# Gates of 16 expert blocks applied where they are built, gate loads on the rows' queue, the gathered tile's remainder 48 rows later

## The chip, the core and the metric

The kernel runs on one core of a Trainium2 chip. The metric is device time in microseconds, the median of several executions. DVE is VectorE, ACT is ScalarE, PE is TensorE, POOL is GpSimd and SP is SyncE, an engine that here only issues transfers.

## The reference, cut to what matters

One decoder block over 512 tokens of 1024 values: a mixer (gated DeltaNet and mLSTM heads), cross-attention into 256 memory tokens, and a PEER layer, each added to the stream, then a last RMSNorm. The change touches the PEER layer alone. It picks for each token and each of 8 heads 16 of 128 x 128 = 16384 single-neuron experts, and computes

```
sc       = q . sub_keys                                  (two halves of 128 keys per head)
top 16 of each half -> 256 candidates -> top 16: expert_id, best_v
gate     = softmax(best_v)                               per head, 16 values
act      = gelu(u[expert_id] . h)                        u: 16384 x 1024, exact gelu
out      = sum over the 128 picked experts of gate * act * v[expert_id]
result   = rmsnorm(x + out) * norm_final_w
```

## The kernel before, in words

The 512 tokens are four tiles of 128. The mixer and the attention run on all tiles (to about 640 us). In the PEER layer the tiles are treated in two ways at the same time.

**Two gathered tiles (0 and 1; G0 in the code).** For each of its 128 slots (8 heads x 16 picks) a tile fetches one row of 1024 float32 per token, 512 KB per fetch, with an indirect DMA that POOL issues (`fetch`, L1057). A first pass over both tiles takes rows of u: DVE multiplies each by the tile's `hn` and sums (L1086). A second pass takes rows of v: DVE adds the row, times the slot's weight, into `hn` (L1097, L1099). That is 4 x 128 = 512 rows. `late_` (L1062) says at which slot of the next tile's pass a tile's remainder stands in the text: `weights_` (Gelu on ACT, L1066, and the product with the gates on DVE, L1067) after the u pass, and `close` (L1069) after the v pass. `close` loads x and the norm row on POOL's queue into two of the row buffers (L1072, L191), adds on DVE (L1074), squares on ACT (L1076) and scales on DVE (L1077); the result is stored later (L1106, L1108). Rows are counted here from 0 to 511 in text order, so `close` of the first tile stands after row 256 + 128 + 16 = 400.

**Two dense tiles (2 and 3, 256 tokens).** They take all 16384 experts, in 128 blocks of 128, which form 16 groups of eight (GB). For block n, TensorE multiplies the block of u with the tokens (16 matmuls of 128 x 256, L313), ACT applies Gelu and writes the activation into a slot of `room` (L961, called from `act_`), the activation is multiplied by a gate matrix that is zero where an expert was not picked (`gated`, L986, one DVE instruction of 128 x 2048 for eight blocks), and TensorE adds the block's part of the output into four PSUM banks (eight matmuls of 128 x 512, L989, called from `add`). `room` holds six groups, so activations run 47 blocks (AHEAD) ahead of additions.

The gate matrices are made tile by tile in 16 calls of `build` (L926), one for 16 tokens: DVE makes one-hot operands, TensorE multiplies them (L942), ACT copies the result into one of two stage buffers (L943) and stores it to DRAM (`gates_`, L944). They come back in groups of eight blocks into one of three buffers `gb` that lie in the same memory as the stages (`gates_of`, L981, issued by SP).

**The dense loop** (`peer_dense`, L963, L1004) has 128 steps e. Step e computes the activation of block e + 47 while there is one (steps 0 to 80), adds block e, issues the loads of a later row block of u (`in_pt`) and of v (`in_pv`), 512 KB each, on SP's queue into nine shared buffers, and runs some rows of the two gathered tiles: 3.3 per step (ROWS_BOTH) up to step 80 and 1.6 (ROWS_DOWN) after. Before the loop stand the first gate loads and `gated(0)` and `gated(1)`; group g + 2 is gated at step 8g + 5.

**What stands before the loop** is written out by hand in ORDER_XA (L56): u, t, T are routing of the dense tiles, b and B the two tiles' eight builds each, aN runs N activations ahead of the loop (47 in all), pN runs N rows of the gathered tiles (167 in all).

**What sets the order.** The text gives each engine's work and its priority; the compiler's planner then puts each instruction into its engine's stream by its own estimate of when operands and buffers are ready. An engine executes its stream strictly in order. Semaphores between the streams are all that holds at run time.

Of the kernel before, what the change touches and what calls it, by code (L numbers as in the profile page):

```python
# [6 lines left out]
F32 = mybir.dt.float32  # L7
# [5 lines left out]
OP = mybir.AluOpType  # L13
# [3 lines left out]
P = 128  # L17
# [11 lines left out]
K = 16  # L29
NSL = PH * K  # L30

ROWS_BOTH, ROWS_DOWN = 3.3, 1.6
NKEY = 128

GSCALE = 2.0 ** 15
# [20 lines left out]
ORDER_XA = ("w2 n0 q008 n1 s0 x0 s1 x1 q104 o0 w1 i0 q148 f0 f1 r6 "  # L56
            "f2 s2 p2 f3 s3 p4 x2 p3 r3 p2 r3 k0 x3 p4 o1 p8 i1 e0 R3 p4 R3 p2 R4 k1 "
            "u0 p5 u1 p5 u2 p5 a1 u3 p5 a2 "
            + "t2 p4 a1 " * 4 + "t2 p4 a5 " + "b1 p5 a1 T2 " * 4 + "b1 p5 a1 T2 a4 d0 " + "b1 p5 a2 " * 3
            + "B1 p5 a1 " * 8 + "a2 p3 " * 6)  # L60


class Phase:
# [12 lines left out]
def _body(ctx, tc, A, out, dbg):  # L76
    from contextlib import ExitStack
    nc = tc.nc
    V, SC, PE, G = nc.vector, nc.scalar, nc.tensor, nc.gpsimd

    def pool(name, bufs=1, **kw):
        return ctx.enter_context(tc.tile_pool(name=name, bufs=bufs, **kw))

    per = pool("per", 2)
    dram = pool("dram", 1, space=bass.MemoryType.DRAM)
# [831 lines left out]
    T = len(DENSE) * P  # L917
    NLD = 9
    TG, TS = 16, 8
    GB = 8  # L920
    NROOM = 6
    AHEAD = NROOM * GB - 1

    gates_ = dram.tile([NKEY // GB, P, T // TG, GB, TG], F32, name="gates_")

    def build(t0, bufs, stage, bank):  # L926

        for s in range(0, TG, TS):
            ts = slice(t0 + s, t0 + s + TS)
            oj, oi, og = hot(bufs())  # L930
            key = [slot[:, x, ts].rearrange("p (a q) -> p a q", q=Q).unsqueeze(2) for x in range(2)]
            for o, k in ((oj, key[1]), (oi, key[0])):
                V.tensor_tensor(o, ioq.unsqueeze(1).to_broadcast([P, TS // Q, P, Q]),
                                k.to_broadcast([P, TS // Q, P, Q]), op=OP.is_equal)
            gates = slot[:, 2:4, ts].rearrange("p g (a q) -> p g a q", q=Q)
            for a in range(TS // Q):
                V.tensor_tensor(og[:, :, a], oi[:, a].unsqueeze(1).to_broadcast([P, 2, P, Q]),
                                gates[:, :, a].unsqueeze(2).to_broadcast([P, 2, P, Q]), op=OP.mult)
                ps = bank()
                for k in range(Q):  # L940
                    for g in range(2):
                        PE.matmul(ps[:, k], oj[:, a, :, k], og[:, g, a, :, k], start=g == 0, stop=g == 1)  # L942
                SC.activation(stage[:, :, s + a * Q:s + a * Q + Q], ps.rearrange("p t i -> p i t"), AF.Copy, scale=1.0 / GSCALE)  # L943
        nc.scalar.dma_start(gates_[:, :, t0 // TG].rearrange("g p i t -> p g (i t)"),  # L944
                            stage.rearrange("p (g i) t -> p g (i t)", i=GB))

    NHOT = TS * 4 * P

# [6 lines left out]
    room, count_a = [], [0]  # L955

    def place(e):
        return room[e // GB % NROOM][:, e % GB]

# [3 lines left out]
    def peer_dense(wu, psO, psC, rest):  # L963
        h = second.h

        def load(src):
            t = wu.tile([P, D], F32, name="ld", bufs=NLD)
            nc.sync.dma_start(t, src)
            return t

        def loaded_u(e):
            return load(A["pt"][e].rearrange("p a b -> p (a b)")) if e < NKEY else None

        def loaded_v(e):
            return load(A["pv"][e * P:(e + 1) * P, :]) if e < NKEY else None

        gb = up_.rearrange("p a b -> p (a b)").rearrange("p (z c e t) -> p z c e t", z=3, c=T // TG, e=GB)

        def gates_of(g):
            if g < NKEY // GB:  # L980
                nc.sync.dma_start(gb[:, g % 3], gates_[g])  # L981

        def gated(g):

            a = room[g % NROOM].rearrange("p e (c t) -> p c e t", t=TG)
            V.tensor_tensor(a, a, gb[:, g % 3], op=OP.mult)  # L986

        def add(e, v, i, z):
            PE.matmul(outs[DENSE[i]][z], place(e)[:, i * P:(i + 1) * P], v[:, z * 512:(z + 1) * 512],  # L989
                      start=e == 0, stop=e == NKEY - 1)  # L990

        for ti in DENSE:
            outs[ti] = [psO.tile([P, 512], F32, name=f"o{ti}{z}") for z in range(2)]
        gates_of(0)
        us, vs = [], []
        for k in range(2):
            us.append(loaded_u(AHEAD + k))
            vs.append(loaded_v(k))
        for g in (1, 2):
            gates_of(g)  # L1000
        for g in (0, 1):
            gated(g)
        last, steps = [], 0
        for e in range(NKEY):  # L1004
            n = e + AHEAD
            if n < NKEY:
                ps = psC.tile([P, 512], F32, name="pa")[:, :T]
                times(us.pop(0).rearrange("p (a b) -> p a b", a=DB), h, ps)
            v = vs.pop(0)
            if e < NKEY - 1:  # L1010
                for i in range(len(DENSE)):
                    for z in range(2):
                        add(e, v, i, z)
            else:
                last.append((e, v))
            if n < NKEY:
                act_(n, ps)
            if e % GB == 5 and e + 2 * GB < NKEY:
                gated(e // GB + 2)
                gates_of(e // GB + 3)  # L1020
            us.append(loaded_u(n + 2))
            vs.append(loaded_v(e + 2))
            steps += ROWS_BOTH if n < NKEY else ROWS_DOWN
            run(rest, int(steps))
            steps -= int(steps)
        run(rest)

        n = len(DENSE)

        def plain():  # L1030
            return wu.tile([P, D], F32, name="ld", bufs=NLD)
        w = row_(4, plain())
        xs = [load(out[ti * P:(ti + 1) * P, :]) for ti in DENSE]
        junk = plain()
        ss = sm.tile([P, n, 2], F32, name="fss", bufs=1)
        half = [slice(z * 512, z * 512 + 512) for z in range(2)]
        rs = []
        for i, x in enumerate(xs):
            for z, c in enumerate(half):
                for e, v in last:  # L1040
                    add(e, v, i, z)
                V.tensor_tensor(x[:, c], outs[DENSE[i]][z], x[:, c], op=OP.add)
                SC.activation(junk[:, c], x[:, c], AF.Square, accum_out=ss[:, i, z:z + 1])
            if i:
                k = len(rs)
                t = sm.tile([P, n], F32, name="ft", bufs=1)
                V.tensor_tensor(t[:, k:i + 1], ss[:, k:i + 1, 0], ss[:, k:i + 1, 1], op=OP.add)
                r = rstd(t[:, k:i + 1], i + 1 - k, "n" if k == i else f"f{k}", 1.0 / D)
                for j in range(k, i + 1):
                    rs.append(r[:, j - k:j - k + 1])  # L1050
                    for c in half:
                        V.scalar_tensor_tensor(xs[j][:, c], xs[j][:, c], rs[j], w[:, c], op0=OP.mult, op1=OP.mult)
                        nc.sync.dma_start(out[DENSE[j] * P:(DENSE[j] + 1) * P, c], xs[j][:, c])

    def peer_gather(ready, buffer):

        def fetch(table, ids, s):  # L1057
# [1 line left out]
            G.indirect_dma_start(out=row, out_offset=None, in_=A[table],  # L1059
                                 in_offset=bass.IndirectOffsetOnAxis(ap=ids[:, s:s + 1], axis=0))  # L1060
            return row
        late_ = 16  # L1062

        def weights_(ti):

# [14 lines left out]
        act, done, stored = {}, [], []  # L1080
# [10 lines left out]
        for ti in G0:  # L1091
            hn, ids = first.hn[ti], first.ids[first.tiles.index(ti)].rearrange("p a b -> p (a b)")
            for s in range(NSL):
                row = fetch("pv", ids, s)
                w = act[ti][:, s:s + 1]
                if s:
                    V.scalar_tensor_tensor(hn, row, w, hn, op0=OP.mult, op1=OP.add)  # L1097
                else:
                    V.tensor_scalar(hn, row, w, None, op0=OP.mult)  # L1099
                if s == late_:  # L1100
                    if ti == G0[0]:
                        weights_(done.pop())
                    else:
                        stored.append(close(G0[0]))
                if s == 2 * late_ and stored:
                    G.dma_start(*stored.pop())  # L1106
                yield
        G.dma_start(*close(G0[1]))  # L1108
# [13 lines left out]
    t = late.tile([P, 2, DB, 2 * P], F32R, name="dh0")  # L1122
    dh.append({"h": t[:, 0], "l": t[:, 1]})
    t = late.tile([P, 4, D], F32, name="dh1")
# [21 lines left out]
    norm, query, soft, mix, out_, lo, up_ = xattn()  # L1146
    def cut(*ts):
        return [t.bitcast(F16).rearrange("p (h a s) -> p h a s", h=PH, a=K) for t in ts]

    ring, stages = [], [up_[:, 2 * z:2 * z + 2].rearrange("p a b -> p (a b)").rearrange("p (i t) -> p i t", t=TG) for z in range(2)]  # L1150

    def bufs():
        if not ring:
# [30 lines left out]
    for what in ORDER_XA.split():  # L1184
# [37 lines left out]
        elif kind == "e":  # L1222
            t = late.tile([P, 6, D], F32, name="W0")
# [11 lines left out]
        else:  # L1235
            if kind not in flows:
                i, f = {"r": (0, 0), "R": (1, 0), "t": (0, 0), "T": (1, 0), "b": (0, 1), "B": (1, 1)}[kind]
                g = first if kind in "rR" else second
# [7 lines left out]
    for nm in ("KT", "Vm"):  # L1246
        t = cst.tile([P, 2, D], F32, name=nm)
# [64 lines left out]
```

## Time and profile before

| | us |
|---|---|
| device time, median of 3 runs | 1942.05 (1935.58 to 1955.63) |
| the profiled execution's own time | 1938.23 |
| its span, first to last instruction | 1936.2 |
| PE busy in the span | 1695.3 (88%) |
| DVE busy | 1239.8 (64%) |
| POOL busy | 814.4 (42%) |
| ACT busy | 398.0 (21%) |
| moved by DMA | 519.0 MB, mean 268 GB/s |

Busy times are sums over the span and say nothing of the order in which limits follow each other; an engine that waits inside an instruction's queue is idle. The granted TensorE clock was 0.94 of full speed on average.

### The profile page before, as it was taken

The page shows a single profiled execution, that of the slowest core. Times are in us where ns is not written, and L with a number is a line of the kernel's source. Part 1 is how long each engine was busy: PE and PEld are TensorE (multiplying, and loading weights), DVE is VectorE, ACT ScalarE, POOL GpSimd, SP SyncE. Part 2 cuts the span into 40 slices and gives each one's busy share as a digit, 9 for nine tenths or more (in the row PEclk, how much of TensorE's full clock was granted, in tenths as well). Part 3 has the DMA queues.
Part 4 walks back from the last instruction along what each step waited for, and adds up shares of the span by engine and source line. Part 5 has one row for each costly group of instructions (what it writes and reads, how often), then busy time and mean ns, then how long its engine had stood idle before and what let it go on. Part 6 is the DMA issues. An engine that isn't in the chain of part 4 may idle for free.

```text
span 1936.2 us, 21351 instructions
## 1 busy us (share of the span) xinstructions
PE 1695.3 (88%) x7444; PEld 1248.5 (64%) x7444; DVE 1239.8 (64%) x2723; ACT 398.0 (21%) x798; POOL 814.4 (42%) x672
## 2 busy tenths in 40 slices
PE   5999999999799879979969198959987859999997
PEld 3878778777788738868858155636654536665443
DVE  6656754652523998999859776567657757666401
ACT  5443442742442121112222000000000000000000
POOL 2122111232210355481435675567656656666100
PEclk9999999999899999989989599979988979999999
DMA  3111111234534688888999999999999999999842
GB/s 133 61 55 55 45 54 50 67 123 155 168 111 156 237 292 319 328 324 262 340 391 358 381 412 411 409 410 407 409 410 403 410 406 404 408 409 409 302 154 87
DMA packets 169739, 519.00 MB, mean 268 GB/s; under 512 B 15648, under 2 KB 48544, under 8 KB 167584
## 3 DMA queue, kind: packets, MB, share of 16 engines
q0 software_dynamic: 74592, 271.61, 36.1%
q1 hardware_dynamic: 62016, 229.26, 32.3%
q10 hardware_dynamic: 33024, 16.78, 3.0%
q8 instruction: 58, 0.95, 0.2%
q14 instruction: 49, 0.40, 0.1%
HBM read 496.62 MB, written 20.97 MB: 267 GB/s over the span
## 4 chain that ended last, share of the span: by engine, by line
PE 49%; DMA 25%; DVE 15%; issue 5%; POOL 3%; ACT 2%; SPq 0%; DVEq 0%; ACTq 0%; POOLq 0%
PE o L989 13%; PE pj L313 7%; PE pj L271 7%; PE pj L284 6%; PE pa L313 5%; DMA Vm<-in_pv,ids 4%; PE acc L445 4%; DMA wh<-in_pu,ids 3%; DMA wh<-in_pv,ids 3%; PE acc L942 2%; DMA gates__132<-W 2%; DMA row<-in_pv,ids 2%; DMA wl<-in_pv,ids 2%; DMA Vm<-in_pu,ids 2%; DVE W L1086 2%
## 5 line engine op out<-in xcount | busy, mean ns | idle before, releaser
L989 PE MATMUL o<-ld,W 128*128 128x512 f32 x832 | 371.6, 598 | 46.2 <-DVE W L986 36.9
L313 PE MATMUL pa<-dh,ld 128*128 128x256 f32 x1296 | 308.2, 393 | 70.0 <-DMA ld<-in_pt 41.7
L313 PEld LDWEIGHTS pa<-dh,ld 128*128 128x128 f32 x1296 | 255.8, 198 | 142.7 <-issue 79.4
L989 PEld LDWEIGHTS o<-ld,W 128*128 128x128 f32 x832 | 159.5, 192 | 221.4 <-issue 171.4
L221 POOL TENSOR_TENSOR wl<-w,wh 128x1024 fp32r<-128x1024 f32 x38 | 92.4, 2433 | 343.0 <-ACT wh L236 288.8
L313 PE MATMUL pj<-dh,w 128*128 128x256 f32 x704 | 163.8, 387 | 4.8 <-ACT W L961 4.6
L313 PEld LDWEIGHTS pj<-dh,w 128*128 128x128 f32 x704 | 134.9, 195 | 23.5 <-ACT W L961 5.0
L1059 POOL DMA_INDIRECT row<-in_pu,ids x75 | 94.2, 1257 | 102.0 <-DVE row L1086 52.1
L1097 DVE SCALAR_TENSOR_TENSOR dh<-row,act,dh 128x1024 f32<-128x1024 f32 x73 | 93.8, 1284 | 50.4 <-DMA row<-in_pv,ids 47.4
L961 ACT ACTIVATE W<-pa 128x256 f32<-128x256 f32 x65 | 24.6, 382 | 474.0 <-PE pa L313 357.6
L1059 POOL DMA_INDIRECT row<-in_pv,ids x75 | 95.5, 1274 | 51.3 <-DMA W<-in_pv,ids 13.4
L1059 POOL DMA_INDIRECT W<-in_pu,ids x70 | 88.6, 1266 | 65.7 <-DVE W L1086 19.0
L313 PE MATMUL pj<-dh 128*128 128x256 f32 x496 | 114.4, 384 | 1.1 <-ACT W L961 1.1
L1086 DVE SCALAR_TENSOR_TENSOR row<-row,dh 128x1024 f32<-128x1024 f32 x75 | 89.7, 1221 | 33.0 <-DMA row<-in_pu,ids 32.6
L284 PE MATMUL pj<-hT,wh 128*128 128x512 f32 x320 | 109.5, 413 | 0.0
L271 PE MATMUL pj<-wh,hT 128*128 128x512 f32 x320 | 106.1, 404 | 0.4 <-ACT hT L211 0.4
L313 PEld LDWEIGHTS pj<-dh 128*128 128x128 f32 x496 | 94.2, 193 | 13.9 <-ACT W L961 1.5
L1086 DVE SCALAR_TENSOR_TENSOR W<-W,dh 128x1024 f32<-128x1024 f32 x70 | 84.6, 1222 | 13.4 <-DMA W<-in_pu,ids 12.7
L989 PE MATMUL o<-ld,dh 128*128 128x512 f32 x192 | 85.2, 592 | 0.0
L236 ACT ACTIVATE wh<-w 128x1024 fp32r<-128x1024 f32 x56 | 59.3, 1059 | 124.7 <-PE pj L271 64.1
L1059 POOL DMA_INDIRECT wl<-in_pu,ids x42 | 56.7, 1351 | 65.6 <-DVE tv L783 18.6
L1059 POOL DMA_INDIRECT wh<-in_pu,ids x41 | 53.7, 1310 | 44.3 <-DVE wh L1086 24.3
(429 smaller groups left out, 3074.1 us busy)
## 6 DMA issues: line engine op xcount, KB each, us to landing
ld<-in_pv SPq DMA_DIRECT2D x128, 512.0 KB
ld<-in_pt SPq DMA_DIRECT2D x81, 512.0 KB
gates__132<-W ACTq DMA_DIRECT2D x16, 1024.0 KB
W<-gates__132 SPq DMA_DIRECT2D x16, 1024.0 KB
w<-in_pt SPq DMA_DIRECT2D x24, 512.0 KB
dh<-in_pt SPq DMA_DIRECT2D x23, 512.0 KB
w<-in_win SPq DMA_DIRECT2D x20, 512.0 KB
w<-in_pwq SPq DMA_DIRECT2D x16, 512.0 KB
```

The costliest lines, as they stand in the source:

```text
L221: G.tensor_tensor(out, a, hi, op=OP.subtract)
L236: SC.activation(hi, wt, AF.Copy)
L271: PE.matmul(acc[i], a[:, d, i * P:(i + 1) * P], b[:, z], start=d == 0 and m == 0, stop=d == DB - 1 and m == len(pairs) - 1)
L284: PE.matmul(acc[:, :n * P], a[:, d], b[:, d], start=d == 0 and m == 0, stop=d == DB - 1 and m == 2)
L313: PE.matmul(ps, w[:, d], h[:, d], start=d == 0, stop=d == DB - 1)
L445: PE.matmul(ps[:, i], l[:, i], r[:, i], start=True, stop=True)
L942: PE.matmul(ps[:, k], oj[:, a, :, k], og[:, g, a, :, k], start=g == 0, stop=g == 1)
L961: SC.activation(place(e), ps, AF.Gelu)
L989: PE.matmul(outs[DENSE[i]][z], place(e)[:, i * P:(i + 1) * P], v[:, z * 512:(z + 1) * 512], start=e == 0, stop=e == NKEY - 1)
L1059: G.indirect_dma_start(out=row, out_offset=None, in_=A[table], in_offset=bass.IndirectOffsetOnAxis(ap=ids[:, s:s + 1], axis=0))
L1086: V.scalar_tensor_tensor(row, row, 1.0, hn, op0=OP.mult, op1=OP.mult, accum_out=act[ti][:, s:s + 1])
L1097: V.scalar_tensor_tensor(hn, row, w, hn, op0=OP.mult, op1=OP.add)
```

## The change

1. `gates_` holds 14 groups, not 16. Each `build` stores groups 2 to 15 and multiplies the activations of groups 0 and 1, which must then be there, on DVE straight from the stage (two multiplies of 128 values per partition and build). There are three stages instead of two.
2. The gate loads are issued by POOL, not SP. `gated(0)`, `gated(1)` and the gate load ahead of the loop go; the loop's first gate loads are those of groups 2 to 4. Group g is gated at step max(4(g - 2) + 1, 8(g - 5) + 5); from group 7 on that is five steps after the step that makes its last activation, where before it was 29 steps after. The load of group g (5 and up) stands nine steps ahead of its gating, or three steps behind the gating of group g - 3, whichever is later.
3. ORDER_XA has 16 activations ahead of the first tile's builds instead of 12 and 28 instead of 21 ahead of the sixth, 47 in all as before, and 158 rows instead of 167.
4. ROWS_BOTH is 3.5 instead of 3.3, ROWS_DOWN 1.65 instead of 1.6.
5. `late_` is 64 instead of 16, so `weights_` stands 48 rows later, `close` of the first tile after row 448; the result's store stands at slot 96 instead of 32.

```
-ROWS_BOTH, ROWS_DOWN = 3.3, 1.6
+ROWS_BOTH, ROWS_DOWN = 3.5, 1.65
...
-            + "t2 p4 a1 " * 4 + "t2 p4 a5 " + "b1 p5 a1 T2 " * 4 + "b1 p5 a1 T2 a4 d0 " + "b1 p5 a2 " * 3
-            + "B1 p5 a1 " * 8 + "a2 p3 " * 6)
+            + "t2 p4 a1 " * 4 + "t2 p4 a9 " + "b1 p5 a1 T2 " * 4 + "b1 p5 a1 T2 a7 d0 " + "b1 p5 a2 " * 3
+            + "B1 p5 a1 " * 6 + "a1 p9 B1 p5 B1 p5 a6 ")
...
+    NOW = 2
...
-    gates_ = dram.tile([NKEY // GB, P, T // TG, GB, TG], F32, name="gates_")
+    gates_ = dram.tile([NKEY // GB - NOW, P, T // TG, GB, TG], F32, name="gates_")
...
         nc.scalar.dma_start(gates_[:, :, t0 // TG].rearrange("g p i t -> p g (i t)"),
-                            stage.rearrange("p (g i) t -> p g (i t)", i=GB))
+                            stage[:, NOW * GB:].rearrange("p (g i) t -> p g (i t)", i=GB))
+        for g in range(NOW):
+            a = room[g][:, :, t0:t0 + TG]
+            V.tensor_tensor(a, a, stage[:, g * GB:(g + 1) * GB], op=OP.mult)
...
-                nc.sync.dma_start(gb[:, g % 3], gates_[g])
+                G.dma_start(gb[:, g % 3], gates_[g - NOW])
...
-        gates_of(0)
+
+        gate_at = {g: max(4 * (g - NOW) + 1, (g - NROOM + 1) * GB + 5) for g in range(NOW, NKEY // GB)}
+        load_at = {g: max(gate_at[g] - 9, gate_at[g - 3] + 3) for g in range(NOW + 3, NKEY // GB)}
...
-        for g in (1, 2):
+        for g in range(NOW, NOW + 3):
             gates_of(g)
-        for g in (0, 1):
-            gated(g)
...
-            if e % GB == 5 and e + 2 * GB < NKEY:
-                gated(e // GB + 2)
-                gates_of(e // GB + 3)
+            for g, at in gate_at.items():
+                if at == e:
+                    gated(g)
+            for g, at in load_at.items():
+                if at == e:
+                    gates_of(g)
...
-        late_ = 16
+        late_ = NSL // 2
...
-                if s == 2 * late_ and stored:
+                if s == late_ + 32 and stored:
...
-    ring, stages = [], [... for z in range(2)]
+    ring, stages = [], [... for z in range(3)]
```

## Rows read from the trace of the kernel before

**Rows 1.** The page's strip of moved bytes, GB/s in 40 slices of 48.4 us.
```profile
GB/s 133 61 55 55 45 54 50 67 123 155 168 111 156 237 292 319 328 324 262 340 391 358 381 412 411 409 410 407 409 410 403 410 406 404 408 409 409 302 154 87
```

**Rows 2.** Windows of the dense stage: window, length, busy us by engine, clock, DMA.
```profile
core 0: us, PE busy (x) PEld busy (x) DVE busy (x) ACT busy (x) POOL busy (x), PEclk, DMA share, GB/s
1080.00:1300.00 220.00, 156.39 (x508) 100.34 (x505) 149.05 (x228) 8.35 (x22) 141.57 (x108) 0.84 1.02 407
1300.00:1589.00 289.00, 237.16 (x792) 155.54 (x792) 196.32 (x153) 13.42 (x35) 181.29 (x148) 0.91 1.02 408
...
1810.00:1937.00 127.00, 116.05 (x271) 51.11 (x269) 19.00 (x40) 4.58 (x12) 0.54 (x1) 0.97 0.44 146
```

**Rows 3.** Chain that ended last, 1548 us on: start, us, engine and piece.
```profile
1568.10 18.92 DMA wh<-out
...
1588.31 0.03 ACT W L1076
...
1589.78 6.19 PE pa L313 x16
...
1599.40 3.45 PE pa L313 x16
1602.86 3.43 PE o L989 x8
...
1761.25 164.81 PE o L989 x384
```

**Rows 4.** Waits of ACT, 1115 to 1930: who waited for whom, us, times, longest.
```profile
ACT W L1076 <- DVE dh L1074: 39.0, 1, 39.0
ACT act L1066 <- DVE row L1086: 33.1, 1, 33.1
```

**Rows 5.** Waits of PE, 1115 to 1930.
```profile
PE pa L313 <- DMA ld<-in_pt: 41.7, 4, 11.8
PE o L989 <- DVE W L986: 36.9, 1, 36.9
PE pa L313 <- ACT W L961: 28.3, 2, 17.7
PE o L989 <- DMA ld<-in_pv: 9.3, 1, 9.3
```

**Rows 6.** Windows of the last builds and of the wait after them.
```profile
1000.00:1081.00 81.00, 57.02 (x352) 50.82 (x351) 60.23 (x102) 19.76 (x37) 36.29 (x28) 0.80 1.01 360
...
1080.00:1117.00 37.00, 0.40 (x4) 0.11 (x1) 27.27 (x45) 0.69 (x2) 26.41 (x22) 0.50 1.01 388
```

**Rows 7.** Instructions of L1066 and L944: ns min/median/max, first and last start.
```profile
L1066 ACT ACTIVATE act<-act x2: 309/310/311, 1040.5 to 1302.0; 128x128 f32<-128x128 f32 x2
...
L944 ACTq DMA_DIRECT2D gates__132<-W x16: 366/366/580, 882.8 to 1081.1; - x16
```

**Rows 8.** Windows between gatings: rows' DVE updates (L1097), then activations (L961, ACT).
```profile
1400.25:1468.92 68.67, 44.96 (x36) 0.93 1.02 408
1468.92:1539.27 70.35, 46.24 (x37) 0.93 1.02 407
...
1400.25:1468.92 68.67, 3.06 (x8) 0.93 1.02 408
...
1589.30:1937.00 347.70, 10.08 (x27) 0.98 0.81 312
```

**Rows 9.** The page's store queue, and instructions of L986, L1067 and L1072.
```profile
q10 hardware_dynamic: 33024, 16.78, 3.0%
...
L986 DVE TENSOR_TENSOR W<-W,W x13: 2284/2285/2289, 1115.0 to 1758.1; 128x2048 f32<-128x2048 f32 x13
...
L1067 DVE TENSOR_TENSOR act<-act,gt x2: 277/284/292, 1078.8 to 1302.4; 128x128 f32<-128x128 f32 x2
...
L1072 POOL DMA_DIRECT2D wh<-out x1: 577/577/577, 1568.1 to 1568.1; - x1
```

**Rows 10.** Waits of ACT, 860 to 1085.
```profile
ACT W L943 <- PE acc L942: 67.3, 55, 6.1
ACT W L943 <- DMA gates__132<-W: 31.8, 3, 22.2
```

**Rows 11.** Waits of SP's own queue, 1085 to 1620.
```profile
SPq L981 <- DVE W L986: 125.7, 9, 31.2
...
SPq L981 <- DMA gates__132<-W: 16.7, 2, 9.3
```

More of the change, by code (lines that the diff above doesn't have):

```diff
@@ L1148, in cut @@
         return [t.bitcast(F16).rearrange("p (h a s) -> p h a s", h=PH, a=K) for t in ts]
-    ring, stages = [], [up_[:, 2 * z:2 * z + 2].rearrange("p a b -> p (a b)").rearrange("p (i t) -> p i t", t=TG) for z in range(2)]
+    ring, stages = [], [up_[:, 2 * z:2 * z + 2].rearrange("p a b -> p (a b)").rearrange("p (i t) -> p i t", t=TG) for z in range(3)]
     def bufs():
```

## The prediction

> **What bounds the kernel now.** I read the page's strip of moved bytes first: about 410 GB/s from slice 23 to slice 36, little before and after [rows 1]. The stage windows say what that means: from 1080 to 1589 us the DMA engines are full (share 1.02, 407 to 408 GB/s) while TensorE works 156 of 220 and 237 of 289 us; from 1810 us the DMA share is 0.44 and TensorE works 116 of 127 us [rows 2]. So transfers bind first and TensorE binds afterwards, and the question is where one hands over to the other.
>
> The chain of waits gives the seam [rows 3]. Its last transfer is the load of x that `close` (L1069) needs for the first gathered tile (issued at 1568.1, 18.9 us); DVE adds it, ScalarE's square (L1076) starts at 1588.31, and from 1589.78 TensorE runs to the end in pieces of 3.45 us (one product with a row block of u, L313) and 3.43 us (eight additions into the output, L989), the last 164.8 us without the former. From its restart to the end of the span are 1936.2 - 1589.8 = 346.4 us. A square can hold TensorE because ScalarE works in order and its fresh activations (L961) empty the two banks that L313 fills: ScalarE stood 39.0 us before the square and 33.1 us before the earlier Gelu of the weights (L1066) [rows 4], and TensorE stood 28.3 us for ScalarE behind the two. Its other waits in the dense stage are 36.9 us for the first gating and 51.0 us for row loads [rows 5], 116 us in all. They cannot just be subtracted: in the 37 us of the longest the DMA engines moved 388 GB/s [rows 6].
>
> The last thing to read is order. The compiler's planner does not keep the text's order between engines: the Gelu that the text has after the last gate build ran at 1040.5 us, while the last gate store was issued at 1081.1 [rows 7]. Between gatings at 1400, 1469 and 1539 us stand 36 and 37 row updates, the one at an edge counted twice, and 8 activations [rows 8], though the text has 8 x 3.3 = 26 rows there. And the square: the text has `close` after row 400, which is step 70 (167 rows before the dense stage, 3.3 per step), so activation 117. In the trace 27 activations follow it [rows 8], so 101 were done: it stands 16 activations ahead of the text.
>
> **The change, part by part.** The sum is made against the profiled execution: span 1936.2, time 1938.2, which is 3.8 us under the median of the three runs.
>
> Groups 0 and 1 gated at the build. An eighth of the gate stores goes: their queue took 3.0% of the span, 58.1 us, so -7.3 us of DMA time [rows 9]. Two loads of 1.05 MB go; ahead of the square that is one (15 of 16 had been issued by then, now 14 of 14). DVE loses two gatings of 2.29 us and gains 32 small multiplies; the nearest row is 0.284 us [rows 9], so +9.1 - 4.6 = +4.5 us, beside a DVE that is busy 60 of 81 us in that stage [rows 6]; without that room it would be 4.5 us on the rows. What these multiplies wait for is not in the trace: nothing at the low end, and at the high end the 67.3 us that ScalarE waits for the same matmuls [rows 10]. I take 0, since the planner has five row updates per build to put in between. The 36.9 us wait of TensorE goes, and is worth 0: the square is late next.
>
> The third stage buffer ends ScalarE's 31.8 us of waits for gate stores [rows 10]; in that stage the DMA share is 1.01 [rows 6], so no transfer comes sooner: 0. The seven blocks of `ahead` moved before the builds are as many as before in all, and TensorE is busy 57 of 81 us there: 0. Nine rows move from before the dense stage into it; the sum below counts rows through, so 0.
>
> Gate loads on POOL's queue. SP stood 125.7 us for gatings with the row loads behind it [rows 11]; TensorE's 51.0 us go, again 0 at the seam. POOL issues 14 loads; its own direct load took 0.577 us [rows 9], 8.1 us together, beside POOL's 142 busy of 220 us. In front of the first loads POOL must wait for the last gate store as SP did, 16.7 us [rows 11], with row fetches queued behind: between 0 and 16.7 us. I take 2, since the nearest window, with that same wait in it, moved 388 instead of 408 GB/s for 37 us. Against the move speaks the Trainium skill, SBUF — State Buffer, section SBUF: two separate sides: a transfer issued from GpSimd can wait for its descriptors while VectorE holds the ports they share. By that rule each of the 14 issues could wait out a gating of 2.29 us, 32 us of POOL's time, which would still fit its idle time; no row here isolates it.
>
> Gating earlier in the text: the trace has gatings right behind their activations already [rows 8], so 0. The weights' Gelu 48 rows later in the text: it was put where its rows were ready, and I expect that again: 0. If it were not, TensorE's stall behind it would only turn into a longer one at the square.
>
> The `close` after row 448 instead of 400 is the edit that counts, for it moves the seam. The square comes 48 rows of 0.524 MB later, 25.2 MB, and with it come two loads (1.05 MB) for every activation that now precedes it. How many activations will precede it? The text has row 448 at step 84 (158 rows before, 3.5 per step to step 80, then 1.65), activation 131, behind the last; 16 ahead of that is 115. By the pace instead: the dense stage starts with 48 activations at about row 156 (the last build stands behind row 153), and 36 rows per 8 activations less two for a gate load on the same queue are 4.25; (449 - 156) / 4.25 = 69, so 117. I take **116**, 15 more than before.
>
> Then 25.2 + 15.7 - 1.05 = 39.9 MB at 408 GB/s are 97.7 us; with -7.3 and +2 the square comes 92.4 us later. TensorE, freed of its early waits, now gets there sooner and stands about 140 us in all (67 activations of 6.88 us from 1082 us on end near 1543). While it stands, only rows flow: 0 lost at the low end (408 GB/s held), 17 us if it moved the 360 GB/s of the window from 1000 to 1081 [rows 6]; I take the 388 GB/s of the next window, 5% or 7 us, since TensorE stands there too. Square: 1588.3 + 92.4 + 7 = 1687.7, restart 1689.2. The rest is 346.4 - 15 x 6.88 = 243.2. End of the span **1932.4**, time 1934.4. As the profiled run lay under the median, I put the result at **1936 us**: no difference that can be told (1% of 1942 is 19 us, about what runs of this kernel tell apart).
>
> The Trainium skill, DMA: Bandwidth & Descriptors, section Specifications, puts a core's share of HBM near 358 GB/s; by that the 39.9 MB would take 111 us and the end would be 1946. The trace holds 407 to 410 GB/s for hundreds of us, so the measurement decides.
>
> Each activation more or less ahead of the square is worth 6.88 - 2.57 = 4.3 us of the end, so the count is the forecast.
>
> **Rivals.** *Faster: the square falls behind the last fresh activation*, as the text has it, or nearly (124 or more). Then nothing holds TensorE, and the transfers set the end: of the last 127 us 56% of DMA time was idle, 71 us; less that and 9.9 us of gate traffic, plus one `close` (18.9 us of load) and the 10 us from the last addition to the end, 1936 - 71 - 10 + 29 = 1884 span, **1886**. For it: step 84 is past the last activation, and TensorE no longer waits at the start. Against it: all three orders read above follow readiness and not the text. Chance 0.24.
>
> *Slower: the square moves 48 rows but hardly any activations*, because in the planner's schedule rows run further ahead of TensorE once their queue and the row loads are apart. At 106 activations the end is 1932.4 + 10 x 4.3 = 1975, **1977**; at 101 it is near 2000. It decides from 110 down, where the time is over 1% up. For it: the planner's pace of 36 rows for 8 activations is far above the text's 26, and 5.05 rows per activation instead of 4.4 would give 106. Against it: gate loads now share the rows' queue. Chance 0.16.
>
> *The rest*, 0.10: DVE standing at the new multiplies (up to 67 us before the dense stage, slower or same), or the gain of TensorE's waits counting after all (faster).
>
> **How the numbers follow.** The forecast has 0.50: 0.35 within 1%, 0.10 faster, 0.05 slower (119 activations and more, 111 and fewer). With 0.24 + 0.10 + 0.02 faster is 0.36; slower 0.14 + 0.05 + 0.04 = 0.23; same 0.35 + 0.02 + 0.04 = 0.41. The range runs from 1886, the faster rival's time, to 1966, the forecast with both high bounds (+10 and +15) and the first 5 us of the slower rival; about 0.09 lies under it and 0.11 over it. The likeliest case alone has 1915 to 1960.
>
> **What would show it.** Right: a chain that ends its transfers at the load in `close`, a square about 100 us later, TensorE without a wait from there on, and 12 activations behind it; TensorE's waits for the first gating and for row loads gone, its waits for ScalarE longer by about as much. The square behind all activations shows the faster rival, 17 or more activations behind it the slower one. POOL standing long before the gate loads, or DVE at the small multiplies, would show a mis-sized term. Wrong altogether: a DMA share well under 1 between 1100 and 1680 us.

## The result, and the profile after

| | before | after |
|---|---|---|
| device time, median of 20 runs each, us | 1947.03 (1935.02 to 1961.35) | 1933.99 (1921.38 to 1947.10) |
| profiled execution: time, span, us | 1938.23, 1936.2 | 1930.96, 1929.0 |
| moved by DMA, MB | 519.00 | 514.81 |

The ratio after to before is 0.9923, 95% interval 0.9903 to 0.9944: a gain of 0.8%, under the 1% that I called telling. The forecast was 1936 us, the median is 1933.99; the profiled execution ends 3.4 us ahead of the forecast's 1932.4. The median of the kernel before is 5 us higher over 20 runs than over the three that I had, so the gain is 13 us where I had forecast 6.

The end of the chain of waits in the kernel after (start, us, engine and piece) has the form of [rows 3]:

```profile
1642.15 18.31 DMA row<-in_pv,ids
1665.27 1.29 DVE dh L1104
...
1714.90 1.30 DVE dh L1104
1720.14 6.35 PE pa L313 x16
...
1750.58 3.45 PE pa L313 x16
1754.04 164.81 PE o L993 x384
1924.40 1.32 DVE ld L1059 x2
```

The instruction that releases TensorE is `close`'s square on ScalarE (L1083 here):

```profile
L1083 ACT ACTIVATE row<-dh x1: 1056/1056/1056, 1718.7 to 1718.7; 128x1024 f32<-128x1024 f32 x1
```

From 1720.1 us TensorE runs to the end without a stop. One thing differs from [rows 3]: the last transfer in the chain is that of a row and lands at 1660.5 us, not the load in `close`. From there to the square the chain is nearly all DVE, row update (L1104) after row update: DVE was busy 56.7 of these 58.1 us, while the DMA share was 1.02. A row update takes DVE 1.30 us, and at 408 GB/s the 0.524 MB of a row take the transfers 1.29, so two limits lie close together there.

Ahead of the restart TensorE stood. Its waits from 1080 to 1930 us (who waited for whom, us, times, longest), to be read against [rows 5]:

```profile
PE pa L313 <- ACT dh L965: 104.6, 2, 66.2
PE acc L943 <- DVE KT L938: 13.7, 2, 7.7
...
PE o L993 <- DVE W L949: 1.1, 1, 1.1
PE o L993 <- DMA ld<-in_pv: 1.0, 1, 1.0
```

The 36.9 us for the first gating and the 51.0 us for row loads are gone but for 1 us each, and the wait for ScalarE rose from 28.3 to 104.6 us: 38.4 at the weights' Gelu, 66.2 at the square. 116 us of waits before, 122 after (13.7 of them in the last builds). What ScalarE itself waited for in that stretch names the two holders, the instructions that keep TensorE waiting (L1073 is the Gelu, L1083 the square):

```profile
ACT KT L1083 <- DVE dh L1081: 86.6, 1, 86.6
ACT row L1083 <- DVE dh L1081: 81.5, 1, 81.5
...
ACT act L1073 <- DVE row L1093: 54.6, 1, 54.6
```

The first of these is the second tile's square at the very end. How many activations stand on each side of the first tile's, the windows of L965 on ScalarE show (window, length, busy us and count, clock, DMA share, GB/s):

```profile
1718.60:1929.00 210.40, 2.55 (x7) 0.97 0.76 289
```

Seven follow the square at 1718.67 us, so 121 of the 128 precede it; before it was 101. The stages, to be read against [rows 2, 6]:

```profile
860.00:1000.00 140.00, 121.42 (x656) 106.57 (x655) 116.95 (x270) 33.15 (x66) 61.78 (x45) 0.91 0.85 298
1000.00:1081.00 81.00, 68.31 (x380) 56.64 (x378) 62.29 (x113) 17.46 (x34) 33.01 (x25) 0.94 0.99 355
1080.00:1117.00 37.00, 19.47 (x91) 12.91 (x92) 35.42 (x65) 5.56 (x10) 28.62 (x20) 0.68 1.01 368
1080.00:1300.00 220.00, 191.18 (x692) 127.18 (x692) 138.99 (x218) 14.75 (x34) 135.54 (x103) 0.93 1.02 398
1300.00:1589.00 289.00, 261.87 (x906) 174.68 (x907) 189.16 (x169) 15.41 (x41) 194.94 (x147) 0.94 1.02 407
1589.00:1690.00 101.00, 64.94 (x223) 42.10 (x221) 70.10 (x55) 2.68 (x8) 65.93 (x54) 0.84 1.02 407
...
1810.00:1929.00 119.00, 108.84 (x254) 48.02 (x252) 30.40 (x50) 4.04 (x10) 11.37 (x10) 0.98 0.55 197
```

The DMA engines are full from 1000 to beyond 1690 us, also while TensorE stands (66 us before 1720.1; the transfers moved 405 GB/s in them, share 1.02). The stretch that lost most is the first, the builds: the kernel before has share 0.94 and 333 GB/s there:

```profile
860.00:1000.00 140.00, 128.48 (x718) 113.74 (x719) 124.34 (x266) 35.93 (x71) 57.46 (x46) 0.95 0.94 333
```

### The profile page after: what moved, and what is told of

It reads as the page before. It is cut to its first block, busy times and chain, and to the rows that moved or that the text cites. A ratio compares the mean times of both kernels' runs of the same rounds, so it can differ in the third digit from the quotient of the medians.

```text
span 1929.0 us, 21360 instructions
## 1 busy us (share of the span) xinstructions
PE 1686.6 (87%) x7444; PEld 1245.9 (65%) x7444; DVE 1244.0 (64%) x2753; ACT 397.8 (21%) x798; POOL 839.0 (43%) x686
## 2 busy tenths in 40 slices
DMA packets 165355, 514.81 MB, mean 267 GB/s; under 512 B 15616, under 2 KB 44416, under 8 KB 163456
## 4 chain that ended last, share of the span: by engine, by line
PE 42%; DMA 26%; DVE 20%; issue 5%; POOL 4%; ACT 2%; DVEq 0%; SPq 0%; POOLq 0%; ACTq 0%
PE o L993 9%; PE pj L271 7%; DMA row<-in_pv,ids 7%; PE pj L313 6%; PE pj L284 6%; PE acc L445 4%; DMA W<-in_pv,ids 3%; DVE dh L1104 3%; PE acc L943 3%; DVE W L1093 2%; DMA wl<-in_pu,ids 2%; DMA row<-in_pu,ids 2%; DMA W<-in_pu,ids 2%; DMA Vm<-in_pu,ids 2%; DMA KT<-in_pv,ids 2%
## 5 line engine op out<-in xcount | busy, mean ns | idle before, releaser
L313 PE MATMUL pa<-dh,ld 128*128 128x256 f32 x1296 | 299.5, 385 | 105.2 <-ACT dh L965 104.6
L313 PEld LDWEIGHTS pa<-dh,ld 128*128 128x128 f32 x1296 | 250.2, 194 | 174.1 <-ACT dh L965 106.3
L313 PE MATMUL pj<-dh,w 128*128 128x256 f32 x704 | 167.8, 393 | 4.5 <-ACT W L965 4.5
L1066 POOL DMA_INDIRECT W<-in_pu,ids x71 | 94.4, 1329 | 97.1 <-DVE W L1093 44.5
L1066 POOL DMA_INDIRECT row<-in_pu,ids x74 | 97.4, 1316 | 83.1 <-DVE row L1093 36.9
L1104 DVE SCALAR_TENSOR_TENSOR dh<-row,act,dh 128x1024 f32<-128x1024 f32 x72 | 92.5, 1284 | 57.2 <-DMA row<-in_pv,ids 56.4
L1066 POOL DMA_INDIRECT row<-in_pv,ids x74 | 99.7, 1348 | 47.0 <-DMA W<-in_pv,ids 20.1
L965 ACT ACTIVATE W<-pa 128x256 f32<-128x256 f32 x65 | 24.9, 383 | 401.9 <-PE pa L313 396.4
L1066 POOL DMA_INDIRECT wh<-in_pu,ids x41 | 64.3, 1567 | 33.2 <-DVE wh L1093 8.5
L1066 POOL DMA_INDIRECT wl<-in_pu,ids x42 | 49.8, 1186 | 66.1 <-DVE tv L783 18.6
## 6 DMA issues: line engine op xcount, KB each, us to landing
gates__132<-W ACTq DMA_DIRECT2D x16, 896.0 KB, 12.3
```

Source lines behind the costliest of these rows:

```text
L313: PE.matmul(ps, w[:, d], h[:, d], start=d == 0, stop=d == DB - 1)
L965: SC.activation(place(e), ps, AF.Gelu)
```

## The experiments

**Theory.** The end is the time of `close`'s square on ScalarE plus what TensorE has left then: 346.4 us with 101 activations ahead of it, 6.88 us less for each one more. **Rivals:** the transfers set the end (then the square's engine wouldn't matter but for its place), or TensorE's waits for row loads and gatings count by themselves. In parentheses behind each title stands the kernel that the edit is made to. What is given as measured is the ratio to the kernel before, with its 95% interval, and the span of the profiled run; "ahead" counts the activations that ScalarE does before the first tile's square. A holder, below, can also be a transfer at the head of a queue.

**1. The remainder where it was** (after, the other parts of the change kept).

```
-        late_ = NSL // 2
+        late_ = 16
...
-                if s == late_ + 32 and stored:
+                if s == 2 * late_ and stored:
```

> The changed kernel with the remainders back at slot 16: close after row 400. In the compiled order 110 activations stand before the square of close (121 in the changed kernel). Theory of the seam (the time at which close's square runs on ScalarE, plus what TensorE has left then, is the end): from the changed kernel's square at 1718.7 us, 48 rows less are -61.7 us and 11 activations less -28.3 us of transfers, square near 1629; left are 208.9 + 11 x 6.88 = 284.6; span near 1915, ratio to before 0.985 to 0.990, faster than the whole change. Rival 'waits' (the gain is that TensorE no longer waits early for gates and row loads, and that ScalarE stalls less): a remainder 48 rows earlier makes ScalarE stall longer, span 1929 to 1945, ratio 0.992 or above. Rival 'traffic' (the gain is the 4.2 MB of gates that are not moved): no difference to the changed kernel, 0.992.

Measured: 0.9836 [0.9803, 0.9868], span 1915.8: the theory's span, and a ratio just under its range. The square came at 1629.33, 110 activations ahead. So the edit that I called the one that counts made the kernel 0.9% slower; the rest of the change gains 1.6%. (`late_` moves the weights' Gelu and the result's store with `close`.)

**2. The remainder later, alone** (before, the same two lines the other way round).

> The kernel before with the remainders at slot 64 alone. In the compiled order 112 activations stand before the square (101 before), at row 449 instead of 401. Theory of the seam: square at 1588.3 + (25.2 + 11 x 1.05 MB)/408 GB/s = 1678, more if transfers are less full while TensorE stands longer; left are 346.4 - 11 x 6.88 = 270.7; span 1950 to 1970, ratio 1.007 to 1.017, slower than before. Rival 'waits': the ScalarE waits move behind, 0 to 28 us gained, ratio 0.985 to 1.0. Rival 'traffic': no change, 1.0.

Measured: 1.0070 [1.0043, 1.0096], span 1953.9; square at 1682.05, 112 ahead. It costs 0.7% alone, too.

**3. The square off ScalarE** (after).

```
-            SC.activation(junk, hn, AF.Square, accum_out=ss)
+            V.scalar_tensor_tensor(junk, hn, 1.0, hn, op0=OP.mult, op1=OP.mult, accum_out=ss)
```

> The changed kernel with the square of close done by DVE instead of ScalarE (one instruction, 1.3 us on DVE); the compiled order is otherwise the same, and no activation stands behind close any more. Theory of the seam: TensorE's 66 us wait at close goes, its wait of 38 us at the weights' Gelu stays; span near 1929 - 66 = 1863, at the most 1885 if the rows end last; ratio 0.958 to 0.970. Rival 'waits' where a wait at close is only one among waits hidden by full transfers: the transfers are the bound, 1920 to 1930, ratio 0.988 to 0.993. Rival 'traffic': 0.992.

Measured: 0.9674 [0.9642, 0.9707], span 1878.1. TensorE's wait at `close` is gone; what it waits for from 1080 to 1930 us is the Gelu and little else, and the chain's end is now rows:

```profile
PE pa L313 <- ACT dh L965: 38.4, 1, 38.4
PE acc L943 <- DVE KT L938: 14.6, 2, 8.5
```

```profile
1838.39 9.70 DMA Vm<-in_pv,ids
...
1858.75 1.30 DVE dh L1104
1860.07 1.24 DVE dh L1081
1861.33 1.25 DVE KT L1083 x2
```

One instruction on another engine, everything else in the same order, and 51 us of the span are gone. This is the state that the faster rival described (span 1884, by transfers), reached by another way.

**4. The same line in the kernel before.**

> The kernel before with the square of close done by DVE; order otherwise as before. Theory of the seam: TensorE's 17.7 us wait at close goes and everything behind it comes that much sooner, span near 1918, ratio 0.990 to 0.993; the other waits (36.9 us first gating, 51 us row loads, 10.6 us Gelu) stay and now count. Rival 'waits' or 'traffic': transfers stay full to 1589 and nothing moves, ratio 0.998 to 1.002.

Measured: 0.9997 [0.9972, 1.0021], span 1940.5. A miss: this is what the rival 'traffic' gave. The chain of this kernel shows who took over:

```profile
1614.65 2.30 DVE W L986
1616.96 0.33 SPq L981
...
1617.38 10.63 DMA ld<-in_pt
...
1628.15 6.56 PE pa L313 x16
```

A gating (L986) ends, only then can SP issue the next gate load (L981), and the row load that TensorE needs stood behind it on SP's queue. TensorE now works where it stood before, up to 1612 us, then stands 16.3 us and restarts at 1628.2 instead of 1589.8. It is about five activations further by then (312.3 us are left instead of 346.4), so the end is where it was. Two holders stood close together, 40 us apart; taking one away shows the other. That this and not the transfers is the reason is shown by 8.

**5. Gate loads back on SP** (after).

```
-                G.dma_start(gb[:, g % 3], gates_[g - NOW])
+                nc.sync.dma_start(gb[:, g % 3], gates_[g - NOW])
```

> The changed kernel with the gate loads issued by SP again. In the compiled order 115 activations stand before the square of close (121 in the changed kernel), at the same row. Theory of the seam: square at 1718.7 - 6 x 2.57 = 1703, left are 208.9 + 6 x 6.88 = 250; span near 1953, ratio 1.00 to 1.01: the whole gain of the change hangs on the order that the planner makes. A second holder, SP standing for a gating with row loads of u and v behind the gate load, should come back as waits of TensorE for row loads. Rival 'traffic' (two groups less to store and load is the gain): ratio 0.992.

Measured: 1.0036 [1.0010, 1.0062], span 1949.2, as the theory of the seam had it; square at 1698.51, 115 ahead. TensorE's waits for row loads are back:

```profile
PE pa L313 <- DMA ld<-in_pt: 35.0, 4, 13.4
PE o L993 <- DMA ld<-in_pv: 31.1, 4, 12.0
PE pa L313 <- ACT W L965: 25.7, 1, 25.7
```

**6. Gate loads on POOL, alone** (before; the same line the other way round).

> The kernel before with the gate loads issued by POOL, nothing else. In the compiled order 106 activations stand before the square (101 before), at row 401 as before. Theory of the seam: square at 1588.3 + 5 x 2.57 = 1601, left are 346.4 - 5 x 6.88 = 312; span near 1915, ratio 0.987 to 0.993; TensorE's waits for row loads gone, its wait at close about 50 us. Rival 'traffic': ratio 1.0. Rival that POOL as issuer starves the rows (each of 16 loads held, row fetches behind them): ratio above 1.0.

Measured: 0.9855 [0.9825, 0.9884], span 1910.1; square at 1597.55, 106 ahead: the theory's order, and a little more gain than its range. One line does more than the whole change.

**7. No multiplies at the builds** (after; groups 0 and 1 stay ungated, which leaves out part of the computation).

```
-            V.tensor_tensor(a, a, stage[:, g * GB:(g + 1) * GB], op=OP.mult)
+            pass
```

> The changed kernel without the 32 small multiplies of the builds: groups 0 and 1 are left ungated, which leaves that part of the computation out. It prices what DVE does and waits there (28.4 us of waits for ScalarE's copies in the profile of the changed kernel, 9.1 us of work). 124 activations stand before the square (121). If the waits reach the seam: rows some 20 us sooner, square near 1718.7 + 7.7 - 20 = 1706, left 208.9 - 20.6 = 188; span near 1895, ratio 0.972 to 0.980. If they are hidden: square near 1726, span near 1915, ratio 0.983 to 0.987.

Measured: 0.9807 [0.9770, 0.9843], span 1912.3; square at 1722.40, 124 ahead. The ratio lies between the two ranges. Three more activations ahead are 3 x 4.3 = 13 us of the 17 us (span) or 23 us (medians) gained; the multiplies themselves cost 4 to 10 us.

**8. Gate loads on POOL and the square on DVE** (before; the lines of 6 and 3).

> The kernel before with both holders taken away and nothing else of the change: gate loads issued by POOL, the square of close done by DVE. Theory: with close on DVE alone the kernel before had no gain because SP's gate load held the row loads of u behind the gating right after close; with both gone TensorE has no wait after the Gelu of the weights and the transfers of the rows set the end: 1865 to 1885, ratio 0.960 to 0.970, as good as the changed kernel with the square on DVE (0.967) though it moves 4.2 MB more. Rival: the rest of the change (gating at the build, fewer waits at the start, three stages) is needed for it: ratio 0.975 to 0.99.

Measured: 0.9659 [0.9627, 0.9690], span 1880.7, the best median of all, 1878.68 us. Both holders gone, the kernel before is as fast as 3, though it moves 4.2 MB more: the gating at the builds, the order and the row rates aren't needed for it, and the traffic of gates is not what was gained.

**9. A third stage buffer** (on 8).

```
-    ring, stages = [], [... for z in range(2)]
+    ring, stages = [], [... for z in range(3)]
```

> The kernel before with the gate loads on POOL and the square of `close` on DVE, and beside these a third stage buffer; the order of every engine is that of the kernel without the third buffer, only a wait for a store goes. That kernel ran at a ratio of 0.966, span 1880.7, its end set by the transfers of rows. Theory: there TensorE, DVE and ACT stand some 18 us near 1000 us for a gate store, and rows are late from there to the end; without the wait rows come up to 17 us sooner and the end with them: span 1862 to 1876, ratio 0.957 to 0.964. Rival: the DMA engines are full there (share 0.98 from 1000 to 1081 us), so the transfers come no sooner and nothing changes: span 1877 to 1884, ratio 0.964 to 0.968, while the wait of ACT for gate stores falls from about 22 us to under 5.

Measured: 0.9684 [0.9647, 0.9722], span 1874.8: no difference from 8 that can be told. Of ScalarE's waits for gate stores from 860 to 1085 us the two short ones went, 9.3 us together, and the long one stayed, so neither theory can be judged by it. First 8, then 9:

```profile
ACT W L943 <- DMA gates__132<-W: 33.5, 3, 23.8
```

```profile
ACT W L943 <- DMA gates__132<-W: 24.2, 1, 24.2
```

ScalarE from 990 to 1017 us in 9:

```profile
992.08 0.38 ACT L961 ACTIVATE W<-pj 128x256 f32<-128x256 f32 x1
1016.20 0.37 ACTq L944 DMA_DIRECT2D gates__132<-W  x1
1016.67 0.60 ACT L943 ACTIVATE W<-acc 128x512 f32<-128x512 f32 x1 [24.21 <-DMA gates__132<-W]
```

The first thing that ScalarE does after 24 us is to issue a store; the copy into a free stage stands behind that. It is the store's issue that waits, for an earlier store to land: in the trace the two carry the same completion semaphore, the earlier one was issued at 972.8, and its last part landed at 1016.1. A buffer more did not help against that.

**10. The moved activations alone** (on 8).

```
-            + "t2 p4 a1 " * 4 + "t2 p4 a5 " + "b1 p5 a1 T2 " * 4 + "b1 p5 a1 T2 a4 d0 " + "b1 p5 a2 " * 3
-            + "B1 p5 a1 " * 8 + "a2 p3 " * 6)
+            + "t2 p4 a1 " * 4 + "t2 p4 a9 " + "b1 p5 a1 T2 " * 4 + "b1 p5 a1 T2 a7 d0 " + "b1 p5 a2 " * 3
+            + "B1 p5 a1 " * 8 + "a1 p3 " * 5 + "p3 ")
```

> The kernel before with the gate loads on POOL and the square of `close` on DVE, and beside these only the seven activations of the change moved ahead of the builds (16 instead of 12 ahead of the first, 28 instead of 21 ahead of the sixth; 47 in all). No multiplies at the builds, all 16 groups stored, two stages. Open is what lowered the DMA share in the first builds of the changed kernel (0.79 from 860 to 940 us and 0.92 from 940 to 1000, against 0.88 and 1.00 without the change). Theory: the moved activations occupy TensorE and ACT, so that DVE, and with it the fetching of rows, is held: share 0.78 to 0.84 from 860 to 940 us, 1 to 12 us later end, span 1883 to 1893, ratio 0.967 to 0.973. Rival: it is the multiplies and the ungated groups' dependence, and the activations are free: share 0.87 or more from 860 to 940 us, span 1876 to 1883, ratio 0.963 to 0.967.

Measured: 0.9676 [0.9648, 0.9704], span 1874.6. The ratio lies where the two ranges meet, the span under both, and the share, 0.85, between them; the stage's bytes decide. First experiment 8, then this one:

```profile
860.00:940.00 80.00, 68.03 (x378) 59.75 (x377) 68.71 (x171) 19.35 (x39) 25.83 (x22) 0.91 0.88 300
940.00:1000.00 60.00, 60.00 (x340) 53.46 (x339) 54.84 (x99) 16.71 (x32) 31.95 (x24) 1.00 1.00 368
```

```profile
860.00:940.00 80.00, 65.71 (x368) 58.02 (x367) 68.10 (x170) 18.33 (x39) 24.95 (x21) 0.91 0.85 299
940.00:1000.00 60.00, 60.00 (x342) 53.41 (x341) 54.70 (x98) 17.42 (x33) 31.62 (x24) 1.00 0.99 369
```

The bytes per second are the same: the moved activations cost nothing that can be told, and the loss in the builds has other causes.

## Why the prediction was right

**The seam.** The step that carried the forecast was that the end is the square's time plus a remainder of 346.4 - 6.88 x (activations ahead - 101). Six kernels test it (the remainder is the span less the square and the 1.47 us to TensorE's restart in [rows 3]):

| kernel | ahead | square at | remainder by the rule | measured |
|---|---|---|---|---|
| after | 121 | 1718.67 | 208.8 | 208.9 |
| 1 | 110 | 1629.33 | 284.5 | 285.0 |
| 2 | 112 | 1682.05 | 270.7 | 270.4 |
| 5 | 115 | 1698.51 | 250.1 | 249.2 |
| 6 | 106 | 1597.55 | 312.0 | 311.1 |
| 7 | 124 | 1722.40 | 188.2 | 188.4 |

Within 1 us each time, whichever wait TensorE had before the square. That the remainder fits is little more than a count of TensorE's work, since nothing holds it behind the square. That the tie is the cause, and not only a mark, is shown by 3: with the square on DVE 51 us go. TensorE's vanished waits are worth nothing by themselves: 116 us of them before, 122 after, under other names, and kernel 5, with 66 us of waits for row loads, obeys the same rule. I had TensorE standing about 140 us in all; at the Gelu and the square it was 104.6, about five activations of 6.88 us less.

**The count was mis-sized**, 121 for my 116. Two errors in my pace: in the trace after, 74 activations precede row 256 where my count from row 156 on gives 71.5, and its gatings stand 33 rows apart from there on (rows 278, 312, 343, 376, 410, 443), where I had 34. 74 + 193 / 33 x 8 = 121. The 115 that I averaged in, from the lead of the old square over the text, was no guide. Each activation costs the square 2.57 us and gives TensorE 6.88 back: five are +12.9 us at the square and -21.5 us at the end.

**The builds were mis-sized the other way**, and this hid the first error. The square came 31.0 us later than I said; 12.9 us are the five activations. From 860 to 1300 us the changed kernel moved 4.9 + 0.4 + 2.0 = 7.3 MB less than before (the windows shown, against [rows 2, 6]), 17.9 us at 408 GB/s. 2.1 MB of that are the gate stores that no longer exist. Their DMA time fell about as computed (-7.9 us for my -7.3), but I credited it to the square as if the engines were full, and in the builds they were not. 3.6 MB are the multiplies': without them (7) the four stretches from 860 to 1300 us moved 0.7 + 2.4 - 0.6 + 1.1 MB more. The first two of them in 7, where the changed kernel had 272 and 332 GB/s:

```profile
860.00:940.00 80.00, 66.36 (x363) 58.30 (x362) 67.01 (x168) 17.93 (x37) 26.74 (x23) 0.89 0.81 281
940.00:1000.00 60.00, 60.00 (x342) 53.35 (x341) 54.82 (x100) 17.80 (x34) 30.40 (x23) 1.00 1.00 372
```

I had bounded what the multiplies wait for by 0 and 67.3 us and took 0. DVE stood 28.4 us there for ScalarE's copies:

```profile
DVE W L949 <- ACT W L944: 28.4, 13, 12.2
```

Most of it took the place of an old wait, for the same matmuls in the same stretch of the kernel before, which I had not read; 4 to 10 us are left:

```profile
DVE Vm L933 <- PE acc L942: 24.3, 6, 17.6
```

The moved activations cost 0, as taken (10). What the last 1.6 MB, 4 us, are due to stays open.

The 2 us that I had added for POOL's wait are among the 7.3 MB: the window with that wait, 1080 to 1117, moved 368 GB/s where the kernel before had 388, 0.7 MB or 1.8 us. The 7 us for a standing TensorE did not show (405 GB/s while it stood). Summed over the packets of the traces, the changed kernel had moved 401.2 MB by 1589 us and the one before 410.5; the 2 MB beyond the 7.3 went mostly before 860 us, and kernels that share the old order differ as much among themselves there. These 9.3 MB are 22.9 us; less 5.1 us for the 2.1 MB that need not be moved they are 17.8 us, where my sum had -7.3 + 2 + 7 = 1.7. With the 12.9 us this gives 29 of the 31.0 us; the rest I can't assign.

So the number was right by luck: 21.5 us less at the end, from the five activations, met 18.1 us more at the square, most of them from the builds. With either repaired alone the forecast would have been some 20 us off.

**The third stage** I costed at 0 because the DMA engines were full. The price holds, the reason does not: the buffer takes away the short waits and not the long one (9). In the changed kernel ScalarE still stood 15.2 us ahead of a store's issue:

```profile
988.47 0.37 ACTq L945 DMA_DIRECT2D gates__132<-W  x1
...
1021.73 0.37 ACTq L945 DMA_DIRECT2D gates__132<-W  x1
1022.20 1.09 ACT L944 ACTIVATE W<-acc 128x512 f32<-128x512 f32 x2 [15.20 <-DMA ld<-in_pv]
```

The view names a row load, since the semaphore that the copy (L944) checks was by then in use for one. But the issue at 1021.73 stands ahead of the copy, and in the trace it waited for the semaphore of the store issued at 988.47, whose last part landed at 1021.66.

The Trainium skill, DMA: Bandwidth & Descriptors, section Anatomy of one DMA — SWDGE (gpsimd) path, says that a DMA's wait for a semaphore is made by the issuing sequencer before dispatch, and not by the DMA engines. By that the copies behind an issue wait as long as the issue does, and the 24.2 us of 9 and the 15.2 here agree.

**Gate loads on POOL** I put at 0 "at the seam" and at 2 us for their wait. The wait was 12.3 us once (bound 16.7); the 14 issues took what their nearest row said, 0.577 us (least, median and most, in ns):

```profile
L985 POOL DMA_DIRECT2D W<-gates__132 x14: 547/577/594, 1126.7 to 1672.7; - x14
```

So far right. But my text named `close` after row 448 as the edit that counts, and there the step failed, not in the sum but in who pays. Alone, POOL's loads are worth -1.45% (6) and the later remainder costs +0.7% (2); the whole change is -0.77%, so if the parts add up all the rest is about nothing. In 6 the square is 9.2 us later, while five more activations ahead of it take 34.4 us off the remainder. My sum held both edits in one count and could not tell them apart.

Against this move I had weighed the Trainium skill, SBUF — State Buffer, section SBUF: two separate sides, with up to 32 us. The section lets a VectorE instruction with two inputs in SBUF, as a gating is, hold the shared ports only against GpSimd work that reads SBUF, so it does not say that a gate load's issue has to wait. The trace agrees: no issue of the 14 took more than 0.594 us. The row fetches of the changed kernel are another matter (start, us, engine, line); a gating ran on DVE from 1443.88 to 1446.16:

```profile
1440.05 0.94 POOL L1066 DMA_INDIRECT wh<-in_pv,ids  x1 [3.72 <-DVE dh L1104]
1441.30 1.41 POOL L1066 DMA_INDIRECT wl<-in_pv,ids  x1 [0.30 <-issue]
1443.01 1.75 POOL L1066 DMA_INDIRECT wh<-in_pv,ids  x1 [0.30 <-issue]
1445.07 1.90 POOL L1066 DMA_INDIRECT wl<-in_pv,ids  x1 [0.30 <-issue]
1447.27 0.93 POOL L1066 DMA_INDIRECT W<-in_pv,ids  x1 [0.30 <-issue]
```

A fetch's issue that overlaps the gating takes 1.75 or 1.90 us, one beside a row update 1.41, one in DVE's pauses 0.93. So a fetch's issue is slowed by 0.8 to 1.0 us against one in a pause, and not held for the whole gating; no run here shows what slows it. POOL has the room: the DMA share stays at 1.02.

**The rivals.** The slower one needed 110 activations or fewer, 5.05 rows for each; the changed kernel's rows ran 33, not 40, for 8 activations. The faster one asked for 124 or more, and 121 stood there. But its condition was set too low: 7 has 124 ahead, TensorE still stood 65.7 us at the square, and the span is 1912.3. Only with nothing held at the square is its price met, by another way (3 and 8: 1878.1 and 1880.7 for 1884). The weights' Gelu stayed at row 256 as expected, and TensorE's 38.4 us behind it do not show in the remainder. Of the signs that I named, the square came 130 us later and not 100, 7 activations and not 12 stand behind it, and the chain's last transfer is not the load in `close`.

## What to carry to other kernels

Look for the one instruction through which an in-order engine ties two flows together; the end is its time plus what the other flow still has to do, as long as nothing else holds that flow, and every edit is priced by what it puts ahead of that instruction and how much it delays it. Read its place from the compiled streams, not from the text. Where two holders stand at one place, price them together: removing the square alone gave nothing, the queue's holder alone 1.5%, both 3.4%.

## What the runs showed of the hardware that was not expected

A store's issue can hold its engine for the landing of an earlier store, though its data are ready: in all twelve kernels here one issue between 1014 and 1027 us stands 10 to 24 us, and ends when the last part of the store lands that was issued 28 to 44 us earlier under the same completion semaphore. In 9 a spare buffer did not change it. And loads pay for a wait that is not theirs, on the queue they share: in 5 TensorE stood 66 us, eight times, for row loads behind gate loads on SP; with those on POOL, at 0.58 us for an issue, 1.0 us of it is left.

The transfers held 407 to 409 GB/s from 1300 to 1810 us. The Trainium skill, DMA: Bandwidth & Descriptors, section Bandwidth, gives 425 GB/s for a core that streams alone, in loads of 16 MB, and the runs are nearer to that than to the 358 that I weighed.
